# Two transformer blocks on one core: scores of both query tiles in one group, norm broadcasts as transposes, mLSTM scores with zero-padded operands

## The chip, the core and the metric

The kernel runs on one core of a Trainium2 chip, in one launch. The metric is the device time of that launch in microseconds (us), the median of several executions. Five engines work side by side, each with an instruction queue of its own that it takes in order: TensorE (PE in the profile, its weight loads PEld), VectorE (DVE), ScalarE (ACT), GpSimd (POOL) and SyncE (SP, which here issues the weight transfers). They wait for each other through semaphores.

## What is computed

A sequence of 256 tokens of width 1024 passes a first block of two layers (an mLSTM layer, then a layer with banded attention; both also attend to 256 memory tokens) and a second block of two layers (neighbourhood attention beside a gated recurrence, then a short convolution). Each layer ends in a feed-forward net with a convolution. All inputs are fp32. The parts that the change touches, cut from the reference:

```python
def rmsnorm(x, g):                       # 15 broadcasts of such a factor in the kernel
    y = x32 * lax.rsqrt(jnp.mean(x32 * x32, axis=-1, keepdims=True) + EPS)
    return (y * g.astype(jnp.float32)).astype(x.dtype)

def mlstm_chunkwise(q, k, v, ig, logf):  # 4 heads of 192
    ...
    s = jnp.einsum('bhtd,bhsd->bhts', qq, kk) * jnp.exp(d - m_t[..., None])
    num = jnp.einsum('bhts,bhse->bhte', s, vv) + ...

def memory_attention(q, mem, w_kv):      # 4 heads of 64, 256 keys, in both layers of block one
    s = jnp.einsum('bshd,bmhd->bhsm', q, mk).astype(jnp.float32) * (MEM_HEAD_DIM ** -0.5)
    p = jax.nn.softmax(s, axis=-1).astype(mv.dtype)
    return jnp.einsum('bhsm,bmhd->bshd', p, mv).reshape(bsz, seq, MEM_WIDTH)

def band_attention(q, k_pad, v_pad, rel_table):   # 12 heads of 64, causal by chunks of 64
    s = jnp.einsum('bqhd,bkhd->bhqk', qc, kc).astype(jnp.float32) * scale + bias
    p = jax.nn.softmax(s, axis=-1).astype(vc.dtype)
    return jnp.einsum('bhqk,bkhd->bqhd', p, vc)
```

Neighbourhood attention (8 heads of 64) has the same form with 512 keys for each of its two query tiles of 128 tokens.

## The kernel before

Activations lie feature-major: 128 features on the partitions, 256 tokens along the row. Every weight matrix is read from memory in tiles of 128 x 1024 (`load_w`, L105), which ACT rounds to a high part (L114) and DVE completes by a low part (L115); a product of 256 tokens is then three matmuls (L122 to L124; L129, L130 and L154 to L156 are the same in other shapes) for each of eight tiles of 128 rows. These matmuls are called *dense* below; they use all 128 rows and columns of the array, and each is one pass.

Between the dense ones stand small fp32 matmuls, which the trace shows as two passes each:

- **Attention in pairs of heads** (`Pair`, L282). Two heads of 64 share a tile of 128 partitions, head j=0 on rows 0 to 63 and head j=1 on rows 64 to 127. `scores` (L290) computes for each query tile qt and each head a 128 x nk block of scores (L304) with 64 rows of the array, head j into PSUM bank j. For memory and band pairs both query tiles fit side by side into the same two banks (`one`); for the four neighbourhood pairs each query tile has banks of its own. The softmax follows at once for each qt: DVE adds the bias and takes the minimum (L312), ACT takes the exponential (L318), DVE scales (L319, L320). `values` (L324) transposes the weights on TensorE (L334), copies them by ACT (L336) and multiplies by the values (L343): head j fills 64 columns of the array and 64 partitions of one bank.
- **mLSTM heads** (`lstm_scores`, L616). A head of 192 is one tile of 128 rows and one half tile of 64 rows that it shares with its neighbour. Scores are two products for 256 columns (L633) and two for 128 (L636), in each a 128-row and a 64-row one. Ahead of them a product with 4 rows (L622) spreads the running maximum `mx` of the head over all partitions, by the selector `sel`.
- **`spread`** (L215) turns a column of norm factors into a row on all partitions: for each of two token tiles an fp32 product of the broadcast column with the identity (L218), two passes each.

The program's text is not the order of the queues: a scheduler in the compiler's front end places each instruction on its engine by a timeline of its own and fills gaps with whatever is ready. `chain` (L347) and `Fill` give it projections to place between a pair's scores and its values. So two matmuls that stand side by side in the text may have dense ones between them in TensorE's queue; the order of the built program tells.

Of the kernel before, what the change touches and what calls it, by code (L numbers as in the profile page):

```python
# [9 lines left out]
F32 = mybir.dt.float32  # L10
# [3 lines left out]
ALU = mybir.AluOpType  # L14
AX = mybir.AxisListType

P = 128
# [33 lines left out]
def network(ctx: ExitStack, tc: tile.TileContext, a):  # L51
# [163 lines left out]
    def spread(rt, ps):  # L215

        for tb in range(2):
            nc.tensor.matmul(ps[:, tb * P : (tb + 1) * P], rt[:, tb : tb + 1].to_broadcast([P, P]),  # L218
                             ident, start=True, stop=True)

# [61 lines left out]
    class Pair:  # L282
# [7 lines left out]
        def scores(self):  # L290
            if self.prep:
                self.prep()

            self.sc = [[None, None], [None, None]]
            one = sum(self.nkeys) <= 512
            sps = None
            for qt in range(2):
                nk = self.nkeys[qt]
                if sps is None or not one:
                    sps, o = [bank("sc"), bank("sc")], 0  # L300
                for lo, n, kap in self.keys(nk):
                    for j in range(2):
                        r = slice(64 * j, 64 * j + 64)
                        nc.tensor.matmul(sps[j][:, o + lo : o + lo + n],  # L304
                                         self.q[r, qt * P : (qt + 1) * P], kap[r],
                                         start=True, stop=True)
                for j in range(2):
                    sc = self.pool.tile([P, nk], F32, tag="sc", bufs=self.sbufs, name="sc")
                    mn = None
                    for lo, n, b in self.bias(j, qt):  # L310
                        m2 = self.pool.tile([P, 1], F32, tag="mn", bufs=8, name="mn")
                        nc.vector.tensor_tensor_reduce(  # L312
                            out=sc[:, lo : lo + n], in0=sps[j][:, o + lo : o + lo + n], in1=b,
                            scale=-0.125, scalar=3e38 if mn is None else mn, op0=ALU.add,
                            op1=ALU.min, accum_out=m2)
                        mn = m2
                    sm = self.pool.tile([P, 1], F32, tag="sm", bufs=4, name="sm")
                    nc.scalar.activation(sc, sc, AF.Exp, bias=mn, scale=-1.0, accum_out=sm)  # L318
                    nc.vector.reciprocal(sm, sm)  # L319
                    (self.norm or nc.vector.tensor_scalar_mul)(sc, sc, sm)  # L320
                    self.sc[j][qt] = sc
                o += nk

        def values(self):  # L324
# [15 lines left out]
            for kb in range(nkb):  # L340
                q0 = 0 if kb * P < self.nkeys[0] else P
                for j in range(2):
                    nc.tensor.matmul(op[64 * j : 64 * j + 64, q0:S], self.val(kb, j),  # L343
                                     pts[j][:, kb, q0:S], start=kb == 0, stop=kb == nkb - 1)
# [169 lines left out]
    with tc.tile_pool(name="mix0", bufs=1, reuse_waits="tile") as pool:  # L514
# [9 lines left out]
        qk = pool.tile([P, 12, S], F32, name="qk")  # L524

        def qk_step(nt):
            ps = proj_fm(a["w_qk"][nt], x2)
# [8 lines left out]
            for s in (1, 2, 3):  # L536
                nc.vector.scalar_tensor_tensor(out=cv[:, s:], in0=g[:, : S - s], scalar=w(3 - s),
                                               in1=cv[:, s:], op0=ALU.mult, op1=ALU.add)
            return nc.scalar.activation(qk[:, nt], cv, AF.Silu)

# [25 lines left out]
        for tt in range(2):  # L566
# [16 lines left out]
        nc.vector.tensor_tensor(out=rows[:4], in0=gt[:4], in1=bc, op=ALU.subtract)  # L583
        mx = pool.tile([4, S], F32, name="mx")
        nc.vector.tensor_tensor_scan(out=mx, data0=ones[:4, 0:1].to_broadcast([4, S]), data1=rows[:4], initial=0.0,
                                     op0=ALU.mult, op1=ALU.max)
        nc.vector.tensor_tensor(out=rows[32:36], in0=bc, in1=mx, op=ALU.add)
        ps = bank("att")
# [4 lines left out]
        nc.vector.tensor_copy(acol, ps[:, :72].rearrange("p (a b) -> p a b", a=2))  # L593
        sel = pool.tile([4, 4, P], F32, name="sel")
        nc.vector.tensor_copy(sel, ident[:4, :4].unsqueeze(2).to_broadcast([4, 4, P]))

# [19 lines left out]
        def lstm_scores(h):  # L616
            if h % 2 == 0:
                parts = ((slice(0, P), h * 3 // 2), (slice(0, 64), h * 3 // 2 + 1))
            else:
                parts = ((slice(0, P), h * 3 // 2 + 1), (slice(64, P), h * 3 // 2))  # L620
            mb = bank("att")
# [9 lines left out]
            sp = bank("sc")  # L631
            for i, (r, kt) in enumerate(parts):
                nc.tensor.matmul(sp[:, :S], qk[r, 6 + kt, 0:P], qk[r, kt, :],  # L633
                                 start=i == 0, stop=i == 1)
            for i, (r, kt) in enumerate(parts):
                nc.tensor.matmul(sp[:, S:384], qk[r, 6 + kt, P:S], qk[r, kt, P:S],  # L636
                                 start=i == 0, stop=i == 1)
# [756 lines left out]
```

## Time and profile before

| | |
|---|---|
| time, median of 3 runs (lowest to highest) | 1393.1 us (1391.67 to 1395.31) |
| profiled execution: its own time | 1394.08 us |
| profiled execution: span of its instructions | 1392.4 us |
| TensorE busy, weight loads busy | 1366.9 us (98%), 1292.6 us (93%) |
| VectorE, ScalarE, GpSimd busy | 1121.7 us (81%), 828.5 us (60%), 47.8 us (3%) |
| granted TensorE clock, mean | 0.997 of full |

The span runs from the first instruction to the last; 1.7 us of the execution's own time lie around it. Matmuls overlap in the array, and the profile models their ends, so a busy TensorE is not one at its peak: what one matmul costs its neighbours is read from the distances of their starts.

### The profile page before, as it was taken

Reading aid. Unit: us, or ns where it says so; the run is one execution under the profiler, and the core shown is the slowest. Engines: PE = TensorE matmul, PEld = TensorE weight load, DVE = VectorE, ACT = ScalarE, POOL = GpSimd, SP = SyncE. Lnnn points to the kernel's source line nnn. Section 1 sums busy time; section 2 is a strip of 40 time slices with the busy share of each in tenths; the row PEclk is TensorE's granted clock in tenths of the full one; section 3 lists DMA queues with packets and bytes.
Section 4 is the critical chain, followed back from the end, with each engine's and each line's share of the span. In section 5 each row is a group of like instructions: output and inputs, shape, how many; then the busy total and the mean of one; then the engine's idle time right before and its main releaser. Section 6 shows DMA issues by size and latency. Waiting matters only on the chain.

```text
span 1392.4 us, 26901 instructions
## 1 busy us (share of the span) xinstructions
PE 1366.9 (98%) x10512; PEld 1292.6 (93%) x10512; DVE 1121.7 (81%) x2125; ACT 828.5 (60%) x1442; POOL 47.8 (3%) x70
## 2 busy tenths in 40 slices
PE   8999999999999999999998999999999999999997
PEld 7987999998998889999898988799998999999986
DVE  6876799997775858999897976689989898888854
ACT  6755565555565856555556866666664455666643
POOL 0000000000101000000012110000000000000000
PEclk9999999999999999999999999999999999999999
DMA  7753477666645538888884544267778875656563
GB/s 254 249 159 121 145 250 229 229 207 194 216 132 157 182 106 286 272 275 272 269 266 140 185 157 137 92 227 228 229 221 304 308 252 187 197 182 185 181 186 98
DMA packets 79696, 284.19 MB, mean 204 GB/s; under 512 B 8912, under 2 KB 9040, under 8 KB 79440
## 3 DMA queue, kind: packets, MB, share of 16 engines
q1 hardware_dynamic: 78480, 278.67, 61.9%
q0 software_dynamic: 800, 3.15, 0.7%
q8 instruction: 82, 1.34, 0.4%
q10 hardware_dynamic: 288, 0.66, 0.1%
q14 instruction: 46, 0.38, 0.1%
HBM read 281.39 MB, written 1.05 MB: 203 GB/s over the span
## 4 chain that ended last, share of the span: by engine, by line
PE 94%; DVE 3%; ACT 1%; issue 1%; DMA 0%; SPq 0%; POOLq 0%; POOL 0%; DVEq 0%; ACTq 0%
PE ps_acc L122 15%; PE ps_acc L124 15%; PE ps_acc L123 15%; PE ps_sc L122 8%; PE ps_sc L124 7%; PE ps_sc L123 7%; PE ps_acc L129 6%; PE ps_sc L129 3%; PE ps_acc L130 3%; PE ps_sc L304 2%; PE ps_sc L130 2%; PE ps_acc L156 2%; PE ps_acc L154 2%; PE ps_att L343 1%; PE ps_acc L155 1%
## 5 line engine op out<-in xcount | busy, mean ns | idle before, releaser
L114 ACT CAST w<-wraw 128x1024 fp32r<-128x1024 f32 (+2 forms) x438 | 445.6, 1023 | 406.7 <-PE ps_acc L124 157.7
L115 DVE TENSOR_TENSOR w<-wraw,w 128x1024 fp32r<-128x1024 f32 (+2 forms) x438 | 522.6, 1198 | 130.9 <-ACT w L114 127.6
L122 PE MATMUL ps_acc<-x,w 128*128 128x256 f32 (+1 forms) x1560 | 442.9, 285 | 2.0 <-ACT w L114 1.8
L124 PE MATMUL ps_acc<-x,w 128*128 128x256 f32 (+1 forms) x1560 | 442.2, 284 | 2.7 <-DVE w L115 2.7
L123 PE MATMUL ps_acc<-x,w 128*128 128x256 f32 (+1 forms) x1560 | 441.7, 284 | 0.0
L122 PEld LDWEIGHTS ps_acc<-x,w 128*128 128x128 f32 x1560 | 294.8, 189 | 7.5 <-ACT w L114 2.9
L124 PEld LDWEIGHTS ps_acc<-x,w 128*128 128x128 f32 x1560 | 294.7, 189 | 6.5 <-DVE w L115 3.3
L123 PEld LDWEIGHTS ps_acc<-x,w 128*128 128x128 f32 x1560 | 295.8, 190 | 2.8 <-issue 2.7
L122 PE MATMUL ps_sc<-x,w 128*128 128x256 f32 (+1 forms) x840 | 240.5, 286 | 8.5 <-ACT w L114 6.7
L124 PE MATMUL ps_sc<-x,w 128*128 128x256 f32 (+1 forms) x840 | 239.6, 285 | 0.0
L123 PE MATMUL ps_sc<-x,w 128*128 128x256 f32 (+1 forms) x840 | 239.4, 285 | 0.0
L122 PEld LDWEIGHTS ps_sc<-x,w 128*128 128x128 f32 x840 | 160.6, 191 | 10.9 <-ACT w L114 7.3
L123 PEld LDWEIGHTS ps_sc<-x,w 128*128 128x128 f32 x840 | 160.8, 191 | 0.7 <-DVE x L170 0.4
L124 PEld LDWEIGHTS ps_sc<-x,w 128*128 128x128 f32 x840 | 160.7, 191 | 0.3 <-DVE w L115 0.2
L129 PE MATMUL ps_acc<-a,w 128*128 128x512 f32 x374 | 130.8, 390 | 0.0
L450 DVE CUSTOM_DVE_ANT_0 ada<-ada,cvec,vec 128x1024 f32<-128x1024 f32 x96 | 121.9, 1278 | 0.7 <-DMA ada<-w_ada 0.6
L130 PE MATMUL ps_acc<-a,w 128*128 128x256 f32 x374 | 105.7, 283 | 1.3 <-DVE w L115 1.3
L129 PE MATMUL ps_sc<-a,w 128*128 128x512 f32 x242 | 84.9, 390 | 0.0
L129 PEld LDWEIGHTS ps_acc<-a,w 128*128 128x128 f32 x374 | 70.2, 188 | 14.5
L389 DVE SCALAR_TENSOR_TENSOR cv<-g,vec,cv 128x255 f32<-128x255 f32 (+1 forms) x176 | 82.8, 476 | 0.4 <-ACT cv L387 0.3
L130 PEld LDWEIGHTS ps_acc<-a,w 128*128 128x128 f32 x374 | 70.6, 189 | 2.3 <-DVE w L115 2.0
L130 PE MATMUL ps_sc<-a,w 128*128 128x256 f32 x242 | 68.2, 282 | 0.0
(370 smaller groups left out, 1917.3 us busy)
## 6 DMA issues: line engine op xcount, KB each, us to landing
wraw<-w_up SPq DMA_DIRECT2D x176, 512.0 KB, 4.3
ada<-w_ada SPq DMA_DIRECT2D x96, 512.0 KB, 4.8
wraw<-w_dn SPq DMA_DIRECT2D x64, 512.0 KB, 4.3
wraw<-w_ev SPq DMA_DIRECT2D x44, 512.0 KB, 3.7
wraw<-w_dn SPq DMA_DIRECT2D x32, 384.0 KB, 3.9
wraw<-w_od SPq DMA_DIRECT2D x24, 512.0 KB, 4.5
wraw<-w_qk SPq DMA_DIRECT2D x12, 512.0 KB, 4.4
wraw<-w_aout SPq DMA_DIRECT2D x8, 512.0 KB, 3.5
```

Of the source, the lines that this page charges most:

```text
L114: nc.scalar.copy(hi[:, c], raw[:, c])
L115: nc.vector.tensor_tensor(out=lo[:, c], in0=raw[:, c], in1=hi.bitcast(F32)[:, c], op=ALU.subtract)
L122: nc.tensor.matmul(ps, w.h[:, c], x.h[:, kt, :n], start=first, stop=False)
L123: nc.tensor.matmul(ps, w.h[:, c], x.l[:, kt, :n], start=False, stop=False)
L124: nc.tensor.matmul(ps, w.l[:, c], x.h[:, kt, :n], start=False, stop=last)
L129: nc.tensor.matmul(ps, w.h[:, c], x.both[:, :, kt, :n], start=first, stop=False)
L130: nc.tensor.matmul(ps[:, 0], w.l[:, c], x.h[:, kt, :n], start=False, stop=last)
L154: nc.tensor.matmul(ps, x.l[:, kt, t], v.h[:, c], start=kt == 0, stop=False)
L156: nc.tensor.matmul(ps, x.h[:, kt, t], v.l[:, c], start=False, stop=kt == 7)
L304: nc.tensor.matmul(sps[j][:, o + lo : o + lo + n], self.q[r, qt * P : (qt + 1) * P], kap[r], start=True, stop=True)
L389: nc.vector.scalar_tensor_tensor(out=cv[:, so], in0=g[:, si], scalar=conv(i, ft), in1=cv[:, so], op0=ALU.mult, op1=ALU.add)
L450: nc.vector.tensor_tensor_reduce(out=out, in0=wt, in1=cvec[j], scale=1.0, scalar=col("ada_b", 48 * l + n), op0=ALU.mult, op1=ALU.add, accu ...
```

## The change

Three edits, and one reordering. (1) `Pair.scores` issues the scores of both query tiles first and the softmax of all four blocks afterwards, where both tiles share the banks. (2) `spread` asks for a transpose in place of a product with the identity. (3) The mLSTM scores use 128 rows throughout: the shared half tiles of q are written into a zeroed tile `qz`, each half in a slot of its own with zeros in the other 64 rows, and `mx` and `sel` get 128 partitions, with zeros below. (4) `values` takes head 1 ahead of head 0.

```diff
     def spread(rt, ps):
         for tb in range(2):
-            nc.tensor.matmul(ps[:, tb * P : (tb + 1) * P], rt[:, tb : tb + 1].to_broadcast([P, P]),
-                             ident, start=True, stop=True)
+            nc.tensor.transpose(ps[:, tb * P : (tb + 1) * P], rt[:, tb : tb + 1].to_broadcast([P, P]),
+                                ident)
...
-            for qt in range(2):
-                nk = self.nkeys[qt]
-                if sps is None or not one:
-                    sps, o = [bank("sc"), bank("sc")], 0
-                for lo, n, kap in self.keys(nk):
-                    for j in range(2):
-                        r = slice(64 * j, 64 * j + 64)
-                        nc.tensor.matmul(sps[j][:, o + lo : o + lo + n],
-                                         self.q[r, qt * P : (qt + 1) * P], kap[r],
-                                         start=True, stop=True)
-                for j in range(2):
+            first = (0, self.nkeys[0] if one else 0)
+            for qts in ((0, 1),) if one else ((0,), (1,)):
+                sps = [bank("sc"), bank("sc")]
+                for qt in qts:
+                    for lo, n, kap in self.keys(self.nkeys[qt]):
+                        o = first[qt] + lo
+                        for j in range(2):
+                            r = slice(64 * j, 64 * j + 64)
+                            nc.tensor.matmul(sps[j][:, o : o + n],
+                                             self.q[r, qt * P : (qt + 1) * P], kap[r],
+                                             start=True, stop=True)
+                for qt, j in [(qt, j) for qt in qts for j in range(2)]:
+                    nk, o = self.nkeys[qt], first[qt]
...
-                for j in range(2):
+                for j in (1, 0):
                     nc.tensor.matmul(op[64 * j : 64 * j + 64, q0:S], self.val(kb, j),
                                      pts[j][:, kb, q0:S], start=kb == 0, stop=kb == nkb - 1)
...
+        qz = pool.tile([P, 4, S], F32, name="qz")
+        nc.gpsimd.memset(qz, 0.0)
...
+            if nt in (1, 4):
+                for j in range(2):
+                    r = slice(64 * j, 64 * j + 64)
+                    last = nc.scalar.activation(qz[r, nt // 4 * 2 + j], cv[r], AF.Silu)
+                return last
             return nc.scalar.activation(qk[:, nt], cv, AF.Silu)
...
-        mx = pool.tile([4, S], F32, name="mx")
+        mx = pool.tile([P, S], F32, name="mx")
+        nc.gpsimd.memset(mx, 0.0)
...
-        sel = pool.tile([4, 4, P], F32, name="sel")
-        nc.vector.tensor_copy(sel, ident[:4, :4].unsqueeze(2).to_broadcast([4, 4, P]))
+        sel = pool.tile([P, 4, P], F32, name="sel")
+        nc.vector.tensor_copy(sel, ident[:, :4].unsqueeze(2).to_broadcast([P, 4, P]))
...
-            if h % 2 == 0:
-                parts = ((slice(0, P), h * 3 // 2), (slice(0, 64), h * 3 // 2 + 1))
-            else:
-                parts = ((slice(0, P), h * 3 // 2 + 1), (slice(64, P), h * 3 // 2))
+            own, shared = ((h // 2 * 3, h // 2 * 3 + 1) if h % 2 == 0
+                           else (h // 2 * 3 + 2, h // 2 * 3 + 1))
+            parts = ((own, qk[:, own]), (shared, qz[:, h]))
...
-            for i, (r, kt) in enumerate(parts):
-                nc.tensor.matmul(sp[:, :S], qk[r, 6 + kt, 0:P], qk[r, kt, :],
-                                 start=i == 0, stop=i == 1)
+            for i, (kt, q) in enumerate(parts):
+                nc.tensor.matmul(sp[:, :S], qk[:, 6 + kt, 0:P], q, start=i == 0, stop=i == 1)
```

TensorE's queue in the built programs, at three places. The first is the first memory pair of layer one. Before, its four scores (L304) are an adjoining two and, 28 dense matmuls later, these two, apart:

```order
L124 MATMUL ps_acc<-x_260,w 128x256
L122 MATMUL ps_acc<-x_260,w 128x256
L304 MATMUL ps_sc<-memk,qm 128x256
L123 MATMUL ps_acc<-x_260,w 128x256
L124 MATMUL ps_acc<-x_260,w 128x256
L304 MATMUL ps_sc<-memk,qm 128x256
L122 MATMUL ps_acc<-x_260,w 128x256
```

After, all four of this pair stand behind the last value products of the mLSTM:

```order
L656 MATMUL ps_att<-v_324,ee 128x193
L657 MATMUL ps_att<-v_324,ee 128x193
L304 MATMUL ps_sc<-memk,qm 128x256 x4
L122 MATMUL ps_acc<-x_260,w 128x256
L123 MATMUL ps_acc<-x_260,w 128x256
```

No dense matmul stands between the scores of the two query tiles any more. The second place is the value products (L343) of a band pair, `vvb` being the band's values. Before, head 0 comes first and alone:

```order
L343 MATMUL ps_att<-pT,vvb 64x256
L123 MATMUL ps_acc<-c_4269,w 128x256
L343 MATMUL ps_att<-pT,vvb 64x256
L343 MATMUL ps_att<-pT,vvb 64x128 x2
L124 MATMUL ps_acc<-c_4269,w 128x256
```

After, the four adjoin:

```order
L123 MATMUL ps_acc<-c_4274,w 128x256
L343 MATMUL ps_att<-pT,vvb 64x256 x2
L343 MATMUL ps_att<-pT,vvb 64x128 x2
L124 MATMUL ps_acc<-c_4274,w 128x256
L122 MATMUL ps_acc<-c_4274,w 128x256
```

The dense matmul that stood inside the group has moved out of it. The third is the third mLSTM head, whose score products name only `qk` before (a 128-row and a 64-row one in each row of two):

```order
L649 MATMUL ps_att<-v_322,ee 128x193
L622 MATMUL ps_att<-mx,sel 128x256
L633 MATMUL ps_sc<-qk 128x256 x2
L636 MATMUL ps_sc<-qk 128x128 x2
L124 MATMUL ps_acc<-x_85,w 128x256
```

After, at the same place:

```order
L657 MATMUL ps_att<-v_324,ee 128x193
L631 MATMUL ps_att<-mx,sel 128x256
L642 MATMUL ps_sc<-qk 128x256
L642 MATMUL ps_sc<-qz,qk 128x256
L644 MATMUL ps_sc<-qk 128x128
L644 MATMUL ps_sc<-qz,qk 128x128
L124 MATMUL ps_acc<-x_85,w 128x256
```

Nothing has moved here; every second product takes its query from `qz`.

## Rows read from the trace of the kernel before

**Rows 1.** The page: busy time by engine; the chain that ended last.

```profile
PE 1366.9 (98%) x10512; PEld 1292.6 (93%) x10512; DVE 1121.7 (81%) x2125; ACT 828.5 (60%) x1442; POOL 47.8 (3%) x70
...
PE 94%; DVE 3%; ACT 1%; issue 1%; DMA 0%; SPq 0%; POOLq 0%; POOL 0%; DVEq 0%; ACTq 0%
```

**Rows 2.** Windows: stretch, length, busy PE, PEld, DVE, ACT, POOL, clock, DMA.

```profile
70.00:114.00 44.00, 44.00 (x306) 38.43 (x306) 34.38 (x58) 22.19 (x44) 0.00 (x0) 1.00 0.49 150
376.00:500.00 124.00, 123.91 (x932) 109.61 (x931) 88.99 (x224) 78.79 (x169) 8.12 (x13) 1.00 0.50 158
```

**Rows 3.** Timeline of PE: start, length, line, names, rows*columns, shape, passes.

```profile
118.47 0.28 PE L122 MATMUL ps_acc<-x,w 128*128 128x256 f32 x1
118.68 0.70 PE L304 MATMUL ps_sc<-memk,qm 64*128 64x256 f32 x2
...
119.53 0.29 PE L124 MATMUL ps_acc<-x,w 128*128 128x256 f32 x1
```

**Rows 4.** Timeline of PE: other groups of scores.

```profile
400.69 0.48 PE L304 MATMUL ps_sc<-kk,qq 64*128 64x128 f32 x2
...
376.65 0.70 PE L304 MATMUL ps_sc<-memk,qm 64*128 64x256 f32 x4
...
843.37 0.71 PE L304 MATMUL ps_sc<-nk,nq 64*128 64x256 f32 x4
843.91 0.60 PE L304 MATMUL ps_sc<-ctxk,nq 64*128 64x256 f32 x4
```

**Rows 5.** Timeline of PE: value products of two band pairs.

```profile
438.90 0.87 PE L343 MATMUL ps_att<-pT,vvb 128*64 128x256 f32 x8
...
471.84 0.65 PE L343 MATMUL ps_att<-pT,vvb 128*64 128x256 f32 x2
...
472.73 0.86 PE L343 MATMUL ps_att<-pT,vvb 128*64 128x256 f32 x6
```

**Rows 6.** Timeline of PE: the scores of the mLSTM head h=1.

```profile
81.69 0.28 PE L124 MATMUL ps_acc<-x,w 128*128 128x256 f32 x1
81.89 0.69 PE L622 MATMUL ps_att<-mx,sel 4*128 4x256 f32 x2
82.52 1.32 PE L633 MATMUL ps_sc<-qk 128*128 128x256 f32 x4
83.77 0.90 PE L636 MATMUL ps_sc<-qk 128*128 128x128 f32 x4
...
84.83 0.28 PE L123 MATMUL ps_acc<-x,w 128*128 128x256 f32 x1
```

**Rows 7.** Timeline of PE: a spread, and two transposes of another line.

```profile
173.48 0.61 PE L218 MATMUL ps_att<-ident,rt 128*128 128x128 f32 x4
...
141.53 0.38 PE L698 MATMUL ps_att<-ident,hn 128*128 128x128 f32 x2
```

**Rows 8.** Line 218, its first and last of three groups: passes, length in ns (least, median, most), first and last start.

```profile
L218 PE MATMUL ps_att<-ident,rt x40: 270/275/376, 30.4 to 1385.7; 128*128 128x128 f32 x40
...
L218 PE MATMUL ps_fil<-ident,rt x4: 270/274/275, 388.0 to 388.4; 128*128 128x128 f32 x4
```

**Rows 9.** Timeline of PE, a memory pair's value products; in brackets the idle time before.

```profile
133.86 1.08 PE L343 MATMUL ps_att<-pT,memv 128*64 128x256 f32 x6 [0.66 <-ACT pT L336]
```

**Rows 10.** Windows: a stretch in the layer with the band.

```profile
455.00:465.00 10.00, 10.00 (x83) 9.24 (x80) 8.00 (x21) 9.93 (x12) 0.44 (x2) 1.00 0.24 78
```

**Rows 11.** Windows: behind a norm, and across the transposes of line 698.

```profile
745.00:749.00 4.00, 4.00 (x23) 4.00 (x23) 3.94 (x12) 1.64 (x4) 0.00 (x0) 0.57 0.58 212
749.00:753.00 4.00, 4.00 (x36) 4.00 (x35) 2.08 (x3) 2.79 (x5) 0.00 (x0) 1.00 0.13 16
...
139.00:143.00 4.00, 3.90 (x32) 3.53 (x32) 3.16 (x9) 2.40 (x5) 0.00 (x0) 1.00 0.01 4
```

**Rows 12.** Lines by form, POOL, and line 539.

```profile
L994 POOL MEMSET at<- 128x512 f32 x4 | 2.1, 528 | 32.5 <-PE ps_att L1097 31.6 <-DVE mk L957 0.9
...
L539 ACT ACTIVATE qk<-cc x12: 399/416/420, 40.4 to 85.1; 128x256 f32<-128x256 f32 x12
```

More of the change, by code (lines that the diff above doesn't have):

```diff
@@ L295, in scores @@
             one = sum(self.nkeys) <= 512
-            sps = None
-            for qt in range(2):
-                nk = self.nkeys[qt]
-                if sps is None or not one:
-                    sps, o = [bank("sc"), bank("sc")], 0
-                for lo, n, kap in self.keys(nk):
-                    for j in range(2):
-                        r = slice(64 * j, 64 * j + 64)
-                        nc.tensor.matmul(sps[j][:, o + lo : o + lo + n],
-                                         self.q[r, qt * P : (qt + 1) * P], kap[r],
-                                         start=True, stop=True)
-                for j in range(2):
+            first = (0, self.nkeys[0] if one else 0)
[11 more added lines that the diff above has]
+                    nk, o = self.nkeys[qt], first[qt]
                     sc = self.pool.tile([P, nk], F32, tag="sc", bufs=self.sbufs, name="sc")
@@ L321, in scores @@
                     self.sc[j][qt] = sc
-                o += nk
         def values(self):
@@ L583, in network @@
         nc.vector.tensor_tensor(out=rows[:4], in0=gt[:4], in1=bc, op=ALU.subtract)
-        mx = pool.tile([4, S], F32, name="mx")
-        nc.vector.tensor_tensor_scan(out=mx, data0=ones[:4, 0:1].to_broadcast([4, S]), data1=rows[:4], initial=0.0,
+        mx = pool.tile([P, S], F32, name="mx")
+        nc.gpsimd.memset(mx, 0.0)
+        nc.vector.tensor_tensor_scan(out=mx[:4], data0=ones[:4, 0:1].to_broadcast([4, S]), data1=rows[:4], initial=0.0,
                                      op0=ALU.mult, op1=ALU.max)
-        nc.vector.tensor_tensor(out=rows[32:36], in0=bc, in1=mx, op=ALU.add)
+        nc.vector.tensor_tensor(out=rows[32:36], in0=bc, in1=mx[:4], op=ALU.add)
         ps = bank("att")
@@ L631, in lstm_scores @@
             sp = bank("sc")
-            for i, (r, kt) in enumerate(parts):
-                nc.tensor.matmul(sp[:, :S], qk[r, 6 + kt, 0:P], qk[r, kt, :],
-                                 start=i == 0, stop=i == 1)
-            for i, (r, kt) in enumerate(parts):
-                nc.tensor.matmul(sp[:, S:384], qk[r, 6 + kt, P:S], qk[r, kt, P:S],
+            for i, (kt, q) in enumerate(parts):
+                nc.tensor.matmul(sp[:, :S], qk[:, 6 + kt, 0:P], q, start=i == 0, stop=i == 1)
+            for i, (kt, q) in enumerate(parts):
+                nc.tensor.matmul(sp[:, S:384], qk[:, 6 + kt, P:S], q[:, P:S],
                                  start=i == 0, stop=i == 1)
```

## The prediction

> **What bounds the kernel now.** I read the page first: TensorE is busy 98% of the span and makes 94% of the chain that ended last [rows 1]. Then the windows of the two stretches in which most of the changed matmuls lie: TensorE has no idle time there, while VectorE is busy 34.4 of 44 us and 89.0 of 124 us, ScalarE less [rows 2]. So the kernel is bound by how fast TensorE takes matmul after matmul, and the question is what each small matmul costs it. A busy share does not tell that, so I read starts in the timeline.
>
> A dense matmul of 256 columns starts 0.12 us after the one before it. A single 64-row score of 256 columns between dense ones is different: from the dense start ahead of it to the second dense start behind it pass 119.53 - 118.47 = 1.06 us; less two dense at 0.12 that is 0.82 us, for a group whose own length is 0.70 [rows 3]. So the array charges 0.12 us for going into the half-array shape and back, beyond the length of the group. I use "length plus 0.12" for every such visit. Two things then stand out [rows 4]. A visit of two scores, one for each half of the rows (four passes), has a length of 0.70 too: the halves run at the same time. And a visit of four scores (eight passes) ends 843.91 + 0.60 - 843.37 = 1.14 after its start, so it costs 1.26, where four single visits cost 3.28. A single score of 128 columns costs 0.48 + 0.12 = 0.60; two passes of 128 more columns are thus 0.22, one is 0.11.
>
> **The change part by part.** How the scores stand in the queue is read from the order of the two programs.
>
> *Scores of memory and band pairs.* Before, their 40 scores make 35 visits: 21 single ones of 256 columns, 9 single ones of 128, and 5 of two (three of 256, one of 128, one mixed). That is 21 x 0.82 + 9 x 0.60 + 4 x 0.82 + 0.60 = 26.5 us. After, there are 14 visits: each of the four memory pairs is one visit of four, 1.26; two band pairs are one visit of four with 128 and 256 columns, and four band pairs are two visits, each with the 128 and the 256 columns of one head. The trace has no visit of the last kind. It lies between 0.82 (the 128 columns hidden) and 0.60 + 0.82 = 1.42 (nothing gained); I take the length 0.70 with two more passes of 0.11, which with 0.12 makes 1.04, because in the visit of four each further pass adds just its columns [rows 4]. The visit of four with both widths comes to the same 1.04 (0.22 less in length than 1.26). Sum 4 x 1.26 + 10 x 1.04 = 15.4. Saved: 11.1.
>
> The neighbourhood pairs keep their form, but the new order splits one of their groups of four into two visits that was one: two scores of one half are 0.70 + 4 x 0.11 + 0.12 = 1.26 each, so one more visit costs 1.3. Left: 9.8.
>
> *Values.* Before, five groups are cut after head 0's first product: three band pairs, two neighbourhood pairs. The rows show one: 0.65 + 0.12 and 0.86 + 0.12 against 0.87 + 0.12 for the whole group [rows 5], 0.76 more. After, none is cut: 5 x 0.76 = 3.8.
>
> *mLSTM scores.* One head takes 84.83 - 81.69 = 3.14 us, less two dense 2.90 [rows 6]. It changes shape four times. After, all ten passes use 128 rows, and the padded half costs no more passes than the 64-row one: six of 256 columns at 0.22 and four of 128 at 0.11, 1.76. Saved 1.14, four times: 4.6. The bound from below is nothing, if such passes keep the length that L622 has (0.69 for two).
>
> *Spreads.* The queue has 60 passes of them in three groups (40, 16 and 4), four to a spread, so 15 spreads [rows 8]. Four passes have a length of 0.61, two transposes 0.38 [rows 7], both in dense surroundings: 0.23 each, 3.4 in all. The Trainium skill (TensorE: Matmul & The Clock Gate, Part 4: PE-mode transpose) gives about 275 ns for one transpose in a kernel. Taken as its cost, two would be 0.55, about a tenth more than a spread costs now, and the sum below would be 5 us smaller; the 0.38 for two in [rows 7] shows that they overlap, and I go by that.
>
> *What costs nothing.* The two memsets on GpSimd: half the size of `qz` takes 0.53 us there, GpSimd is busy 47.8 us in all, and the first SiLU, whose output they must precede, starts at 40.4 [rows 1, 12]; without that cover they would cost 1.3. Two SiLU instructions become four of 64 rows, as long as the whole ones at most, 0.42 each [rows 12], 0.8 us on ScalarE in a stretch of some 40 us in which TensorE does not wait. `sel` copies the same columns.
>
> *Waits.* In the first memory pair TensorE stood 0.66 us until the second head's weights were copied, head 0 having gone ahead [rows 9]. In the new order 19 dense matmuls (2.3 us) stand between the last transposes and the values: that wait goes, and head 0 isn't cut off, 1.1 saved. But in the second memory pair and the third neighbourhood pair the values now stand right behind the transposes with nothing between; head 1 waits there for the last copy, about 0.6 each, and all dense matmuls behind it in the queue wait as well. I count the two against the one: zero.
>
> There is one stretch in which faster matmuls can't help. From 455 us ScalarE is busy 9.93 of 10 us [rows 10], by the gates of the context on top of the weight casts, and VectorE is nearly so behind it. The weights of the dense matmuls come from there. About 1.7 us of the savings (two visits of scores and one group of values) fall into these 10 to 15 us; I write them off.
>
> **Sum.** 9.8 + 3.8 + 4.6 + 3.4 - 1.7 = 19.9 us, against the profiled execution's 1394.1: 1374.2. The median of the runs is 1.0 lower than that execution, so about 1373.
>
> **Rivals.**
>
> *Weight preparation takes half of it.* With 10 us less in the 124 us of the band layer, VectorE's 89.0 would be 78% and ScalarE's 78.8 69% [rows 2]; with 4.6 less in the first stretch VectorE's 34.4 would be 87%. If bursts like that at 455 sit in most of these, TensorE waits for casts instead, and some 10 us come back: 1383. Against it: TensorE's idle time in the 124 us is 0.1 now. Chance 0.11.
>
> *The passes keep their price.* Padded products and transposes may not overlap as the rows around suggest; then only the grouping pays, 9.8 + 3.8 - 1.7 = 11.9: 1381. Chance 0.06.
>
> *The clock falls: slower.* Behind one norm, after TensorE had stood still, its clock was 0.57 of full in a window of 4 us, and 23 matmuls ran in it against 36 in the next 4 us: 13 x 0.12 = 1.6 us lost [rows 11]. If the clock fell so at each spread because transposes keep the array less busy, 15 spreads would lose 24 us: 1397. The change would end slower from 13 such falls on (13 x 1.6 = 20.8). The page section named above says that transposes do not hold the clock as matmuls do. Against it, from rows: four microseconds in which transposes of line 698 alternate with dense matmuls ran at 1.00 [rows 7, 11]. Chance 0.02.
>
> *The scheduler's other order eats it.* VectorE's and ScalarE's queues also change in the first feed-forward net and the neighbourhood layer, where nothing was meant to. New waits of 16 us or more would leave no change; the two new ones that I found are 0.6 each. Chance 0.03.
>
> *It pays more.* No loss at 455, no new wait, the 1.1 kept, and the visits of one head at their lower bound: 19.9 + 1.7 + 1.1 + 1.8 = 24.5, 1369; two or three us more if the queue's regularity also spares waits for weights: 1366. Chance 0.06.
>
> **How the numbers follow.** The forecast has the rest, 0.72. Its own bounds are the visits of one head (8 x -0.2 to +0.4, so -1.8 to +3.0), the waits (-1 to +2) and the burst (0 to 3): 1369 to 1379. For the range I reach to the rivals at 1366 and 1381: 1366 to 1382. A difference of 0.3%, 4.2 us, is about what a measurement of this kernel can tell from none. Faster: all but the clock and the scheduler's order, 0.95; same 0.03; slower 0.02.
>
> **What would show it.** In the profile of the changed kernel the memory pairs' scores are one merged entry of eight passes, some 1.1 long; the mLSTM scores of a head take 1.8 from dense to dense; a spread is two passes, 0.38 long; the first memory pair's values begin with no idle time, the second's with about 0.6. The layer with the band ends some 17 us earlier than before, and the rest of the program keeps its length but for the spreads. I would be wrong if idle time for weights (ScalarE, line 114; VectorE, line 115) grew by more than 5 us, or if the clock fell behind more than the one norm.

## The result and the profile after

The changed kernel takes 1373.78 us (median of 4 runs, 1372.97 to 1375.08), the kernel before 1393.21 us on the same chip: a ratio of 0.986, with a 95% interval of 0.9846 to 0.9874. The profiled execution took 1373.04 us, its span is 1371.3 us, 21.1 less than before.

The page of the changed kernel, where the two lines of [rows 1] stood: busy time by engine, and the chain that ended last.

```profile
PE 1342.9 (98%) x10482; PEld 1283.1 (94%) x10482; DVE 1119.4 (82%) x2125; ACT 829.9 (61%) x1444; POOL 51.0 (4%) x72
...
PE 93%; DVE 2%; ACT 2%; DMA 1%; issue 1%; SPq 0%; POOLq 0%; POOL 0%; DVEq 0%; ACTq 0%
```

TensorE's busy time fell by 24.0 us and the span by 21.1: nearly all of the gain was time in which TensorE worked, and 3 us of it came back as idle time. The bound has not moved. The two stretches of [rows 2], begun and ended within about 1 us of where the same work begins and ends now (columns as there):

```profile
70.00:110.00 40.00, 40.00 (x308) 38.77 (x307) 34.12 (x57) 23.58 (x50) 0.00 (x0) 1.00 0.56 172
366.00:482.00 116.00, 115.74 (x935) 107.03 (x934) 87.61 (x224) 78.78 (x170) 9.41 (x13) 1.00 0.54 170
```

They are 4 and 8 us shorter. VectorE and ScalarE do as much as before in less time, and TensorE waits 0.26 us in them.

**Scores.** TensorE's timeline at three places, with the dense neighbours where there are any: a memory pair, one head of a band pair, and one of the neighbourhood groups that the new order splits.

```profile
108.75 1.13 PE L304 MATMUL ps_sc<-memk,qm 64*128 64x256 f32 x8
...
393.02 0.28 PE L124 MATMUL ps_acc<-x,w 128*128 128x256 f32 x1
393.23 0.92 PE L304 MATMUL ps_sc<-kk,qq 64*128 64x128 f32 x4
...
394.30 0.28 PE L122 MATMUL ps_acc<-x,w 128*128 128x256 f32 x1
...
821.38 0.28 PE L124 MATMUL ps_acc<-x,w 128*128 128x258 f32 x1
821.60 0.70 PE L304 MATMUL ps_sc<-nk,nq 64*128 64x256 f32 x2
822.13 0.59 PE L304 MATMUL ps_sc<-ctxk,nq 64*128 64x256 f32 x2
...
822.88 0.28 PE L123 MATMUL ps_acc<-x,w 128*128 128x258 f32 x1
```

Four scores of a memory pair are one entry of eight passes, 1.13 us long (1.14 forecast). The visit of one head, a form that the trace before did not have, costs 394.30 - 393.02 less two dense matmuls, 1.28 - 0.24 = 1.04. The one of the neighbourhood costs 1.50 - 0.24 = 1.26. Both are the prices of the prediction to the hundredth.

**mLSTM.** The head h=1, as in [rows 6]:

```profile
79.41 0.29 PE L124 MATMUL ps_acc<-x,w 128*128 128x256 f32 x1
79.54 0.60 PE L631 MATMUL ps_att<-mx,sel 128*128 128x256 f32 x2
79.98 0.59 PE L642 MATMUL ps_sc<-qk 128*128 128x256 f32 x2
80.41 0.59 PE L642 MATMUL ps_sc<-qz,qk 128*128 128x256 f32 x2
80.84 0.38 PE L644 MATMUL ps_sc<-qk 128*128 128x128 f32 x2
81.06 0.39 PE L644 MATMUL ps_sc<-qz,qk 128*128 128x128 f32 x2
81.21 0.36 PE L122 MATMUL ps_acc<-x,w 128*128 128x256 f32 x1
81.41 0.28 PE L123 MATMUL ps_acc<-x,w 128*128 128x256 f32 x1
```

From 79.41 to 81.41 less two dense matmuls it is 1.76 us, as forecast, where it was 2.90. Starts stand 0.43 to 0.44 apart for 256 columns in two passes and 0.22 for 128, with no step between whole and padded operands.

**Values.** The band pair that [rows 5] shows cut, now whole, then the first two memory pairs and the second and third neighbourhood pairs; in brackets the idle time ahead and who ended it.

```profile
456.88 0.87 PE L343 MATMUL ps_att<-pT,vvb 128*64 128x256 f32 x8
...
123.58 1.08 PE L343 MATMUL ps_att<-pT,memv 128*64 128x256 f32 x8
...
127.41 0.38 PE L334 MATMUL ps_att<-ident,sc 128*128 128x128 f32 x2
128.25 1.08 PE L343 MATMUL ps_att<-pT,memv 128*64 128x256 f32 x8 [0.46 <-ACT pT L336]
129.27 0.44 PE L706 MATMUL ps_att<-ident,hn 128*128 128x128 f32 x2
...
836.83 1.08 PE L343 MATMUL ps_att<-pT,nv 128*64 128x256 f32 x8 [0.39 <-ACT pT L336]
...
854.10 1.08 PE L343 MATMUL ps_att<-pT,nv 128*64 128x256 f32 x8 [0.68 <-ACT pT L336]
```

The wait of the first memory pair [rows 9] is gone; the two that were foreseen are there with 0.46 and 0.68 us, and one of 0.39 that was not. But these three take no time from the kernel. In the kernel before, the second memory pair stood so:

```profile
137.02 0.38 PE L334 MATMUL ps_att<-ident,sc 128*128 128x128 f32 x2
137.33 1.61 PE L343 MATMUL ps_att<-pT,memv 128*64 128x256 f32 x8
138.87 0.33 PE L698 MATMUL ps_att<-ident,hn 128*128 128x128 f32 x1
```

From its transposes to the next product it took 138.87 - 137.02 = 1.85 us, without idle time ahead and with longer values; now it takes 129.27 - 127.41 = 1.86. The two neighbourhood pairs, from the start ahead of their values to the second start behind them, took 2.70 and 3.03 us before and take 2.72 and 3.04 now.

**Weights.** What TensorE waited for, from the view of waits: sum, times, longest.

```profile
PE ps_sc L122 <- ACT w L114: 6.7, 4, 5.3
PE ps_acc L124 <- DVE w L115: 3.2, 5, 1.5
PE ps_acc L122 <- ACT w L114: 2.0, 5, 0.4
...
PE ps_acc L130 <- DVE w L115: 1.3, 1, 1.3
```

For ScalarE's casts it waits 8.7 us in all (8.5 before), for VectorE's low parts 4.5 (4.3 before).

**Where the time came from, stage by stage.** Every kernel here has the same 9608 dense matmuls, and but for exchanges over short distances (many of them in e7) in the same order, so the start of the k-th of them can be compared from kernel to kernel. The table has how much earlier than before a stage ended, less how much earlier it began (us; positive is gained). Stages are named by their time in the kernel before; the columns e1 to e9 are the experiments below. The 18 us at the start hold no edited instruction; the last dense matmul starts at 1382.0, and what stands behind it is outside the table.

```
before us   after     e1     e2     e3     e4     e5     e6     e7     e8     e9
0-18        +0.93  +0.66  +1.95  +0.43  +1.32  +1.70  +1.07  -0.45  +0.94  +1.02
18-115      +4.38  +0.21  -0.44  +4.63  +0.03  +4.39  +2.85  +4.39  +4.36  +4.40
115-142     +4.32  +0.02  +4.31  +0.04  -0.02  +4.36  +4.31  +4.30  +4.33  +4.32
142-379     +0.04  +0.45  -0.46  -0.01  -0.01  +0.01  +0.02  -4.67  +0.03  +0.02
379-553    +10.71  +0.37  +8.31  +0.00  +2.49  +8.67 +10.73 +15.60 +14.63 +10.71
553-727     +0.01  +0.00  +0.00  +0.00  +0.00  +0.00  +0.00  -6.89  +0.08  -0.00
727-748     +0.43  +1.43  +0.03  +1.84  +1.40  +1.43  -1.02  +1.29  +0.81  -1.97
748-773     +0.01  +0.01  +0.01  +0.00  +0.00  +0.01  +0.00  +0.03  -0.49  -0.30
773-907     +0.56  +0.77  +0.00  +0.01  +0.97  +0.85  +0.58  +5.27  +4.91  -0.68
907-1033    +0.19  +0.19  +0.00  +0.00  +0.00  +0.19  +0.19  -1.17  +0.18  +0.18
1033-1112   -1.05  -0.00  -0.30  +0.01  -0.07  -0.68  -0.16  -2.83  +0.00  -0.07
1112-1382   +0.26  +0.11  +0.00  -0.14  -0.02  +0.26  +0.25  -1.42  +0.24  +0.26
all         20.79   4.21  13.42   6.81   6.09  21.18  18.82  13.44  30.02  17.92
```

Four rows scatter where an edit cannot have done it: 0-18, the norm at 727-748 and the 25 us behind it, and 1033-1112. What e9 shows of the norm and of 1033-1112 is told there; for 0-18 the cause stays open. "Outside the scatter" below means the sum over the other eight rows; for the changed kernel it is 20.5.

### The profile page after: what moved, and what is told of

Its sections match the earlier page's. It is cut to its first block, busy times and chain, and to the rows that moved or that the text cites. A ratio compares the mean times of both kernels' runs of the same rounds, so it can differ in the third digit from the quotient of the medians.

```text
span 1371.3 us, 26850 instructions
## 1 busy us (share of the span) xinstructions
PE 1342.9 (98%) x10482; PEld 1283.1 (94%) x10482; DVE 1119.4 (82%) x2125; ACT 829.9 (61%) x1444; POOL 51.0 (4%) x72
## 3 DMA queue, kind: packets, MB, share of 16 engines
HBM read 281.39 MB, written 1.05 MB: 206 GB/s over the span
## 4 chain that ended last, share of the span: by engine, by line
PE 93%; DVE 2%; ACT 2%; DMA 1%; issue 1%; SPq 0%; POOLq 0%; POOL 0%; DVEq 0%; ACTq 0%
PE ps_acc L124 15%; PE ps_acc L122 15%; PE ps_acc L123 14%; PE ps_sc L124 7%; PE ps_sc L122 7%; PE ps_sc L123 7%; PE ps_acc L129 6%; PE ps_sc L129 4%; PE ps_acc L130 3%; PE ps_sc L130 2%; PE ps_sc L304 2%; PE ps_acc L156 1%; PE ps_acc L154 1%; PE ps_acc L155 1%; PE ps_att L343 1%
## 5 line engine op out<-in xcount | busy, mean ns | idle before, releaser
L122 PEld LDWEIGHTS ps_sc<-x,w 128*128 128x128 f32 x840 | 160.3, 191 | 10.8 <-ACT w L114 7.3
```

Of the source, the lines that this page charges most:

```text
L122: nc.tensor.matmul(ps, w.h[:, c], x.h[:, kt, :n], start=first, stop=False)
```

## Experiments

The theory is the prediction's: each visit of the half-array shape costs 0.12 us beyond its length, and padded products and transposes cost only their columns. The rivals are that the gain comes through fewer waits or another order in the queues, and that one part alone (the grouping) pays while the others keep their price. Each part was first made alone.

### e1: spreads as transposes, alone

```diff
-            nc.tensor.matmul(ps[:, tb * P : (tb + 1) * P], rt[:, tb : tb + 1].to_broadcast([P, P]),
-                             ident, start=True, stop=True)
+            nc.tensor.transpose(ps[:, tb * P : (tb + 1) * P], rt[:, tb : tb + 1].to_broadcast([P, P]),
+                                ident)
```

> The kernel before with the spreads as transposes, nothing else. Theory (each edit saves the passes and shape changes that it takes out of TensorE's queue, and the parts add up): 15 spreads at 0.23 us, 3.4 us faster, about 1389.8; in the trace two passes to a spread, 0.38 us long. Rival (the gain comes from the rearranged queue as a whole, with fewer waits, and a transpose costs what its length says): 15 x 0.1 us slower, about 1394.7.

Measured: 1389.83 us against 1392.73, ratio 0.9984 (0.9975 to 0.9993). Outside the scatter the table has 2.1 us for 11 spreads (two more lie at the norm, one at 1110, and the last, at 1385, behind the table's end). The spread of [rows 7], in its surroundings:

```profile
172.50 0.28 PE L123 MATMUL ps_sc<-x,w 128*128 128x256 f32 x1
172.62 0.38 PE L218 MATMUL ps_att<-ident,rt 128*128 128x128 f32 x2
...
172.96 0.28 PE L123 MATMUL ps_acc<-x,w 128*128 128x256 f32 x1
```

From dense start to second dense start it takes 0.46 us, where the matmul form took 0.68: 0.22 saved. Spreads between dense matmuls give 0.19 to 0.23 each (rows 18-115, 142-379, 907-1033). The one at 1110 gives nothing (the next dense matmul starts 0.53 us behind the spread's start before, 0.54 now), and the one at 545, behind a wait for the norm factor, about 0.14. The one behind the table's end gives the full price: from the last dense matmul to the end of the span pass 10.08 us, 10.36 before. With it e1 has 2.4 us that can be read.

### e2: scores of both query tiles in one group, alone

```diff
-            for qt in range(2):
...
+            for qts in ((0, 1),) if one else ((0,), (1,)):
+                sps = [bank("sc"), bank("sc")]
+                for qt in qts:
```

> The kernel before with the scores of both query tiles in one group, nothing else. Theory: a visit of the half-array shape costs 0.12 us beyond its length, and the two halves of the rows run at once in it; 35 visits of memory and band scores become 14 longer ones: 11.1 us less, about 1382. Rival (only the number of shape changes counts, the halves don't gain from standing together): 21 visits fewer at 0.12 us, 2.5 us, about 1390.7.

Measured: 1380.76 us, ratio 0.9911 (0.9897 to 0.9924). Outside the scatter 11.7 us, 4.3 with the memory pairs of layer one and 8.3 with layer two; the -0.4 and -0.5 in the rows ahead of these are scores of the second query tile, which now stand with the first ahead of the stage's border. The grouping is the main part, and about as large as the visits say. But some 0.9 of the 11.7 is no visit: with head 0 still first, the first memory pair's values no longer wait (from the dense matmul ahead of them to those behind, 0.9 us less). The wait of [rows 9] went through the earlier scores.

### e3: mLSTM scores on 128 rows, alone

```diff
...
-                nc.tensor.matmul(sp[:, :S], qk[r, 6 + kt, 0:P], qk[r, kt, :],
-                                 start=i == 0, stop=i == 1)
+                nc.tensor.matmul(sp[:, :S], qk[:, 6 + kt, 0:P], q, start=i == 0, stop=i == 1)
...
```

> The kernel before with the zero-padded mLSTM operands, nothing else. Theory: a head goes from 2.90 to 1.76 us of TensorE time, 4.6 us in all, about 1388.6. Rival (twice the rows cost what the shape changes saved, or ScalarE's two further instructions and the memset come through): no change, 1393.

Measured: 1387.76 us, ratio 0.9961 (0.9949 to 0.9974). The stage of the mLSTM gains 4.63 us, 1.16 a head, and no other does outside the scatter: the padded products do not keep their price.

### e4: head 1 first in the values, alone

```diff
-                for j in range(2):
+                for j in (1, 0):
                     nc.tensor.matmul(op[64 * j : 64 * j + 64, q0:S], self.val(kb, j),
```

> The kernel before with head 1's values ahead of head 0's, nothing else. Theory: head 1's weights are the last to arrive, so the group waits once and is not cut; five cut groups become whole at 0.76 us, less about 0.6 us of new waits at two groups that stand right behind their transposes: 3 us faster, about 1390. Rival (what the cut lost, the later start loses too): no change, 1393.

Measured: 1388.75 us, ratio 0.9976 (0.9967 to 0.9985); 3.4 us outside the scatter. The three band pairs give 2.5 of it. Of the two neighbourhood pairs that were cut the first gives 0.76 and the second 0.2, since TensorE there waits 0.28 us for VectorE (`x`, line 170) where head 0's product stood. The first memory pair now waits 1.23 us ahead of its values, and row 115-142 stays as it was: that wait takes nothing, and its pair gains nothing either.

### e5: the whole change, with head 0 first again

```diff
-                for j in (1, 0):
+                for j in range(2):
                     nc.tensor.matmul(op[64 * j : 64 * j + 64, q0:S], self.val(kb, j),
```

> The changed kernel with head 0's values ahead again, the rest as changed. Theory: five groups of values are cut again, 5 x 0.76 = 3.8 us; one neighbourhood group of scores is whole again in this order (1.3 us back), and the new waits at two groups of values go (1.2 us): 1 to 3 us slower than the changed kernel, about 1375.5. Rival (the order of the halves is worth nothing): 1373.8.

Measured: 1374.62 us, ratio 0.9879 (0.9862 to 0.9895); the interval overlaps that of the changed kernel. Outside the scatter it gains 18.7 where the changed kernel gains 20.5: head 1 first is worth 1.7 us beside the other edits, 3.4 alone. In the neighbourhood layer, where the changed kernel splits a group of scores, it costs 0.3. By the starts of the dense matmuls the first pair's values give 0.76 there and the fourth's 0.35, and the split takes 1.3; across the waits of 0.39 and 0.68 us nothing changes.

### e6: the whole change, with `mx` and `sel` on 4 partitions

```diff
-        mx = pool.tile([P, S], F32, name="mx")
-        nc.gpsimd.memset(mx, 0.0)
+        mx = pool.tile([4, S], F32, name="mx")
...
-        sel = pool.tile([P, 4, P], F32, name="sel")
+        sel = pool.tile([4, 4, P], F32, name="sel")
```

> The changed kernel with the selector and the running maximum on 4 partitions again, the score products still padded. Theory: one shape change in and out returns in each head, 0.82 instead of 0.43 us: 4 x 0.39 = 1.6 us slower than the changed kernel, about 1375.4. Rival (the padding pays by the score products alone, a single 4-row product hides): 1373.8.

Measured: 1374.76 us, ratio 0.9873 (0.9859 to 0.9888). In TensorE's timeline, the same head:

```profile
79.63 0.28 PE L124 MATMUL ps_acc<-x,w 128*128 128x256 f32 x1
79.84 0.69 PE L630 MATMUL ps_att<-mx,sel 4*128 4x256 f32 x2
80.47 0.70 PE L641 MATMUL ps_sc<-qk 128*128 128x256 f32 x2
```

The 4-row product starts 0.21 us behind the dense one, not 0.13, and the next 0.63 behind it, not 0.44. The two passes have the same columns to stream; 124 zero rows more make them cheaper. The stage gains 2.85 us where the changed kernel gains 4.38: 0.38 a head for this one visit, which is a third of what the padding brings.

### e7: both score banks as one tile, everywhere

If the price is the visit, then asking for both banks at once should keep the four or eight scores of a group together throughout.

```diff
+    def banks():
+        two[0] = psum.tile([P, 2, 512], F32, tag="sc", bufs=1, name="ps_sc")
+        return two[0][:, 0], two[0][:, 1]
...
-                sps = [bank("sc"), bank("sc")]
+                sps = banks()
```

> The changed kernel with the two score banks as one PSUM tile, so that a group of scores starts when both are free; the order of the built program has every group of scores in one piece (bar one). Theory: five neighbourhood groups lose one visit each (5 x 1.26), four band groups one each (about 4 x 0.9), 9.5 us faster than the changed kernel, about 1364. Rival (both banks are now freed together, so other users of these banks and the next scores wait longer, and TensorE stands still): half of it or nothing, 1369 to 1376.

Measured: 1380.01 us, ratio 0.9912 (0.9897 to 0.9926); the expectation failed. The table says where. The stages with attention gain 4.9 (379-553) and 4.7 us (773-907) on the changed kernel, as expected; those without lose 16.4 (4.7 in 142-379, 6.9 in 553-727, and 1.4, 1.8 and 1.7 in the last three; the 1.8 stand in a row that scatters, and there the granted clock was 0.58 from 1094 to 1098 us). In its view of waits:

```profile
PE ps_acc L137 <- ACT w L129: 6.0, 8, 0.9
PE ps_sc L137 <- ACT w L129: 5.6, 1, 5.6
PE ps_acc L139 <- DVE w L130: 4.4, 5, 1.5
...
PE ps_att L233 <- POOL ov L1137: 2.3, 1, 2.3
```

The first line stood at 2.0 us in the changed kernel. In the feed-forward nets and the out-projections the dense products use the two score banks too (the calls of `bank("proj")`), and there the two now come and go together.

### e8: both score banks as one tile, only in the stretches with attention

```diff
+    def wide(w):
+        if rot["pool"]:
+            rot["pool"].close()
+        rot["pool"] = ExitStack()
+        rot["sc"] = rot["pool"].enter_context(tc.tile_pool(
+            name=f"scp{rot['n']}", bufs=1, space=bass.MemoryType.PSUM))
+        rot["wide"] = w
...
-        rot["wide"] = False
+        wide(False)
```

> The changed kernel, with the two score banks as one tile of two banks only in the attention and mLSTM stretches; in the out-projections and feed-forward nets they are two tiles of one bank each again, as in the changed kernel. The built program has 29 visits of the half-array shape where the changed one has 39. Theory (the run before lost its time only because the projections of the feed-forward nets rotate through the score banks): the 9.5 us that merging gained there stay and the 16 us lost elsewhere do not return, 1364 us, bounds 1362 to 1367. Rival (one tile is itself the cost: a softmax holds both banks until its last block is read, also among the pairs): the stretches with attention gain less than 9 us or wait, 1369 or more. The band and neighbourhood stretches should be 4.8 and 4.7 us shorter than in the changed kernel, the feed-forward nets unchanged to 0.5 us each.

Measured: 1364.49 us against 1392.47, ratio 0.9801 (0.9787 to 0.9816), faster than both kernels (the changed one took 1374.6 on the same chip, e9). The stages without attention are as in the changed kernel to 0.1 us outside the scatter, those with it gain 3.9 and 4.4 more, where 4.8 and 4.7 were expected. So e7 lost its time through the banks of the dense products and not through the groups. The four scores of a neighbourhood query tile, which the changed kernel splits at 821.60 above, now stand as one group:

```profile
817.05 0.70 PE L325 MATMUL ps_sc<-nk,nq 64*128 64x256 f32 x4
817.59 0.60 PE L325 MATMUL ps_sc<-ctxk,nq 64*128 64x256 f32 x4
```

Something is left there: the view of waits has one of 2.3 us for GpSimd (`ov`) that the changed kernel has not.

### e9: the changed kernel once more

> The changed kernel once more, unchanged, as a control for what varies from one execution to the next. Time 1373.8 us within 1 us. If the fallen clock behind the norm that follows the first block's last feed-forward net, and the wait for the low parts of a weight near 1085 us, belong to the change, they are there again with 3.4 us at half clock and 0.8 us of idle time. If they only come and go, one of them is missing or of another size here; the first 18 us, which no edit touches, then also differ by up to 2 us between the profiles.

Measured: 1374.6 us (4 runs, 1371.22 to 1377.47), ratio 0.9867 (0.9845 to 0.989). Its first 727 us are those of the changed kernel to 0.1 us in each row; behind them it gains 3.0 us less, by the same program. Three causes show.

*A late transfer ahead of the norm.* GpSimd's timeline and TensorE's, first of the changed kernel, then of its repetition:

```profile
711.45 0.84 POOL L1158 TENSOR_SCALAR rpbt<-rpbt 128x768 f32<-128x768 f32 x1 [0.57 <-DMA rpbt<-rpb]
...
718.79 2.81 POOL L224 TENSOR_TENSOR rt<-v,neghalf 128x2 f32<-128x2 f32 x2
...
721.66 0.43 PE L218 MATMUL ps_att<-ident,rt 128*128 128x128 f32 x2 [0.54 <-POOL rt L224]
```

```profile
713.81 1.00 POOL L1158 TENSOR_SCALAR rpbt<-rpbt 128x768 f32<-128x768 f32 x1 [3.02 <-DMA rpbt<-rpb]
...
722.12 2.38 POOL L224 TENSOR_TENSOR rt<-v,neghalf 128x2 f32<-128x2 f32 x2
...
723.87 1.37 PE L218 MATMUL ps_att<-ident,rt 128*128 128x128 f32 x4 [3.76 <-POOL rt L224]
```

GpSimd works off the bias table `rpbt` of the neighbourhood layer in its queue ahead of the norm factor `rt`. When the transfer `rpb` lands 2.4 us later, `rt` is 3.3 us later, and TensorE stands 3.76 us before the spread. e6 has the same (3.07 and 3.75 us). The dense matmuls behind the norm start 2.0 us later for it, less than the wait grew, since another one, 1.53 us for VectorE, shrinks to 0.2. This is the main part of the -1 to -2 in row 727-748; in the repetition the clock, told next, was also low for longer there (0.50 from 724 to 728 us, 0.68 to 732).

*The clock.* Windows of the changed kernel and of e1 around the same norm, and of the repetition at the neighbourhood values (clock in the third column from the end):

```profile
720.00:724.00 4.00, 1.92 (x15) 1.44 (x14) 3.05 (x6) 3.04 (x5) 1.60 (x2) 1.00 0.78 238
724.00:728.00 4.00, 4.00 (x24) 4.00 (x22) 4.00 (x11) 1.14 (x3) 0.00 (x0) 0.57 0.56 215
```

```profile
740.00:744.00 4.00, 1.92 (x15) 1.44 (x14) 3.05 (x8) 3.85 (x7) 0.79 (x1) 1.00 0.79 255
744.00:748.00 4.00, 4.00 (x36) 4.00 (x35) 4.00 (x12) 2.30 (x5) 0.00 (x0) 1.00 0.40 145
```

```profile
854.00:858.00 4.00, 3.33 (x19) 3.09 (x19) 3.96 (x12) 2.83 (x6) 0.00 (x0) 0.65 0.47 132
```

With the same 1.92 us of busy TensorE ahead, the clock fell to 0.57 of full on the mean of the next 4 us in the one, most of them at 1.2 GHz, and stayed at 2.4 GHz in the other; 24 matmuls against 36 is 1.4 us. Behind this norm it fell in seven of eleven profiles (before, after, e2, e6, e7, e8, e9) and not in e1, e3, e4 and e5. At 854 us it fell in the repetition alone, with 1.2 us lost in row 773-907. That transposes lower it does not show: in e1, where all 15 spreads are transposes, the mean granted clock is 0.998, and 0.997 before.

*A late transfer at 1080 us.* VectorE's timeline of the changed kernel, and of the repetition:

```profile
1081.05 1.28 DVE L450 CUSTOM_DVE_ANT_0 ada<-ada,cvec,vec 128x1024 f32<-128x1024 f32 x1 [1.88 <-DMA ada<-w_ada]
```

```profile
1083.89 1.28 DVE L450 CUSTOM_DVE_ANT_0 ada<-ada,cvec,vec 128x1024 f32<-128x1024 f32 x1 [0.88 <-DMA ada<-w_ada]
```

In the changed kernel the transfer lands 1 us later for VectorE, the low part of the next weight stands behind it in the queue, and TensorE waits 0.78 us at 1084.80. In the repetition that wait is absent: the -1.05 in row 1033-1112 is not the change's.

## Why the prediction was right, step by step

The forecast of 1373 us came true at 1373.8, and the parts made alone show that it did so for its reasons. Outside the scatter e1 to e4 gain 2.1, 11.7, 4.5 and 3.4, together 21.8 us before rounding, the whole change 20.5. The 1.3 between lie mainly in the neighbourhood layer, which gains 0.8 and 1.0 with e1 and e4 and 0.6 with all: that is the visit of 1.26 that the new order splits there, and that neither part alone splits. With the 0.3 of the last spread the whole change has 20.8 us against the forecast's 19.9.

- *Scores of memory and band pairs, 11.1, and one visit more, 1.3.* Confirmed: 11.7 alone, some 10.8 without the wait that went with them. The price of a visit and the one taken between bounds for a single head, 1.04, were right to a hundredth.
- *Values, 3.8.* 3.4 alone: four of the five cut groups gave their 0.76, the last 0.2 to 0.35, because TensorE waits beside it. Beside the other edits it is 1.7, which counts in the split visit that head 1 first brings.
- *mLSTM, 4.6.* 4.5 alone. e6 shows that the products with 4 rows pay like those with 64, since the price is the change of shape.
- *Spreads, 3.4.* Too large: 2.4 can be read. The 0.23 for one is right between dense matmuls (0.19 to 0.23) and behind the last of them (0.28), and wrong as a price for all 15: those at 545 and 1110 us gave 0.14 together, and what the two at the norm behind 727 gave can't be told from the scatter. The figure of the Trainium skill for one transpose (TensorE: Matmul & The Clock Gate, Part 4: PE-mode transpose), about 275 ns, taken as its cost, would have made e1 slower; e1 was faster, with 0.38 us for two.
- *Waits, zero.* Wrong, by 0.9. The one that is gone gave 0.9, and it went by the earlier scores (e2), not by head 1 going first (e4). The two new ones are there as foreseen, with 0.46 and 0.68, and a third of 0.39, but they cost nothing: before, the same groups took the same time from start to start, and the wait lay inside them. To set idle time against idle time was the error; the distances of the starts tell.
- *The burst from 455 us, -1.7.* Wrong. The idle time at the weights in the same work went from 0.1 to 0.26 us; row 379-553 has the whole sum of its visits. That ScalarE is busy 9.9 of 10 us in such a window did not mean that TensorE would wait for it. Weights cast ahead can have covered the 1.7 us; no run shows how many lay ready.
- *Weight preparation as a rival.* It did not take anything: waits for weights went from 12.8 to 13.2 us, and were 12.1 to 12.9 in e1 to e4.
- *The clock as a rival.* It fell where it did before. That it also fell once at 854 us shows that such places exist in the changed kernel, at 1.2 us each and not in each execution.
- *The sign that was named.* The layer with the band ends 19.5 us earlier than before, the first 18 us left out, where some 17 were foreseen: the burst's 1.7 and the wait's 0.9 are about the difference.

The mechanism was right; that the sum came so close is in part luck. The spreads were too large by up to 1.0 and the values by 0.4, the burst and the waits took off 2.6 that did not come, and these partly cancel.

Left open: why the clock falls behind the same wait in one execution and not in another; why e7's dense products wait longest for ScalarE's casts and not for their banks; the last 1.2 us between e8 and its expectation; and what makes the first 18 us differ by up to 2 us between executions.

## What to carry to other kernels

Where one engine is busy throughout, price an edit by distances between starts from neighbour to neighbour, in dense surroundings, and then ask for each instance whether the surroundings are dense; a count times a price was too much for the spreads here (3.4 for 2.4). Idle time ahead of an instruction is not yet time lost: the same group can have waited inside before, and only the distance from start to start shows the difference. Small products in another shape of the array are best asked for together, and padding with zeros to the whole array can be cheaper than leaving rows out. Whether the compiler keeps them together depends on how their output banks are allotted: one tile over both banks did it here (e8), but only where no other work rotates through those banks (e7).

## What the runs showed of the hardware

- A product with 4 rows costs as much beyond its passes as one with 64: 0.38 us a visit here, and 124 rows of zeros take that away (e6).
- Four 64-row scores of 256 columns in two passes each, two per half of the rows, take 1.13 us in one group, where one takes 0.70.
- The granted clock fell behind one and the same norm in seven profiles of eleven; in the changed kernel it did and in e1 it did not, with 1.92 us of work in the 4 us ahead in both, and the fall cost 1.4 us. At 854 us it fell in one of two executions of one program and cost 1.2 us.
- Transfers that land 1 to 2.4 us later in one execution than in another reach TensorE through an engine's queue order: 0.78 us more idle time through VectorE, 3.2 us more through GpSimd, of which 2.0 were lost.
